# A hybrid decoder layer on one core: the order of the last two experts' weights, the last down projection and the last combination

## The chip, the core and the metric

The kernel runs on one core of one Trainium2 chip. The metric is the device time of one execution in microseconds (us); several executions are timed and the median is given. One execution is also recorded by the hardware profiler; times in it count from the start of its span.

## What is computed

One layer of a decoder for 256 tokens of 2048 channels in float32: a modulated norm, a mixer of a gated recurrence and an attention, an output projection, and then a mixture of 32 experts, of which each token uses two. Only this last part is touched:

```python
g_sel = jnp.argmax(g_logits, axis=-1)                 # 1 of 4 groups
top_val, top_idx = lax.top_k(e_in, 2)                 # 2 of its 8 experts
weights = p_group[:, None] * jax.nn.softmax(top_val, axis=-1)
...
hid = jax.nn.silu(xb @ w_gate[e]) * (xb @ w_up[e])    # 2048 -> 512, twice
return hid @ w_down[e]                                # 512 -> 2048
...
y = jax.ops.segment_sum(contrib, tok, num_segments=T)
x = x + g2[:, None, :] * y
```

Every expert's weights are read once: 8 MB for gate and up, 4 MB for down, in float32.

## The kernel before, in words

**Engines.** TensorE (PE) multiplies and transposes, VectorE (DVE) multiplies and adds, ScalarE (ACT) does activations and issues the stores, SyncE (SP) issues the weight loads. Each takes its instructions in the order of its own list. The build makes that order: it goes by the order of the code, but may put an instruction ahead of earlier ones of the code that still have to wait.

**The weight stream.** All weights come in chunks of up to 128 x 4096 floats (2048 KB) through a ring of seven tiles (4 from the start, 2 and 1 added later). `items` is the hand-written order of the chunks, `ring_fill` (line 154) issues the next loads on SP while a tile is free, `ring_get` names a chunk, and `ring_done` (line 172) gives its tile back, so that a next load can be issued once the matmuls that read it are over. For each expert the order is four up chunks ("gu") and two down chunks ("dn"), the latter each with half of the 2048 output columns.

**An expert.** Its tokens (up to 32) have been gathered by `dispatch` (line 915) for four experts at a time, one step of it after each of the first chunks of an up product. The up product (loop from line 997, matmuls at line 1003) takes 16 matmuls of 256 columns for each chunk; four at a time go to four 32-row parts of one PSUM tile. In float32 each matmul is two instructions in the trace. `hidden` (line 964) makes silu(gate) times up on ACT and DVE, transposes it on PE and copies it to the tile `hT`. `down` (line 974, matmuls at 979) makes half of the output columns for 32 tokens: 16 matmuls of 256 columns and then four DVE multiplies of 32 x 256 with the gate's row (line 983), into 32 rows of `Y4`, which holds the rows of four experts.

**The combination.** When the fourth expert of a group has a half of its columns, `combine` (line 950) multiplies the 128 rows of `Y4` by the tokens' weights `PWT` (transposed): for each block j of 512 columns and each half t of the tokens one matmul (line 956) and one addition of 128 x 512 into the running result `accx` (line 958). In the last group each block is stored when both its additions are done, 512 KB on ACT's queue (line 960). Products and combinations share four PSUM tiles ("w").

**Behind it.** A loop (line 1025) for experts with more than 32 tokens follows; the number of its rounds is read by every engine, and there is no work of it in this trace.

Of the kernel before, what the change touches and what calls it, by code (L numbers as in the profile page):

```python
# [17 lines left out]
P = 128  # L18
D = 2048
# buffers: weight ring, 4 KB tiles that live long, 4 and 2 KB temporaries, splits, more ring later  # L20
RING, NARENA, NTEMP, NSPLIT, RING2 = 4, 14, (8, 6), 4, 2
# rows of w_ada for the gates and the second modulation: chunks behind each step of the products
SPREAD = (1, 4, 7, 5, 5, 2, 0, 0, 0, 2, 1, 1, 0)
EARLY = {28: 1}
HEAD = 2  # expert chunks loaded ahead of the last of these rows
AHEAD = 3  # steps of the first dispatch ahead of the first expert
T = 256
NE = 32
# [5 lines left out]
# column offsets of the shape constants  # L34
# [3 lines left out]
# column offsets of the parameters laid out by channel  # L38
# [7 lines left out]
def tile_hybrid_layer(ctx, tc, A, out):  # L46
# [40 lines left out]
    # ---------------------------------------------------------------- constants  # L87
# [15 lines left out]
    # ---------------------------------------------------------------- weight stream  # L103
# [8 lines left out]
    def merge(ws, bs):  # L112
        """Items ws with the items bs spread behind them."""
        done = 0
        for i, w in enumerate(ws):
            items.append(w)
            want = min(len(bs), -(-(i + 1) * len(bs) // len(ws)))
            items.extend(bs[done:want])
            done = want
# [8 lines left out]
    experts = [(k, e, q) for e in range(NE) for k, q in (("gu", 0), ("gu", 1), ("gu", 2), ("gu", 3), ("dn", 0), ("dn", 1))]  # L128
# [3 lines left out]
    def source(it):  # L132
        k = it[0]
        if k == "adt":
            return A["w_ada_t"][it[1]], 4096
        if k == "ada":
            return A["w_ada"][("g1", "sh2", "sc2", "g2").index(it[1]), it[2]], 4096
        if k == "win":
            if it[2] == (0, 1):
                return A["w_in_1"][it[1]], 3328  # L140
            return A["w_in"][it[1], it[2][0] // 2 - 1], 4096
        if k == "qup":
            return A["w_q_up"][it[1]], 3072
        if k == "kvup":
            return A["w_kv_up"][it[1]], 2048
        if k == "wout":
            return A["w_out"][1 - it[1], it[2]], 4096
        if k == "gu":
            return A["w_gu"][it[1], it[2]], 4096
        return A["w_down"][it[1], it[2]], 4096  # L150
# [26 lines left out]
    # ---------------------------------------------------------------- small helpers  # L177
    def log_exp_tables(inst):
        """The table set with both Ln and Exp, loaded behind inst."""
        load = S.preload_act_table_set("natural_log_exp_and_others")  # L180
        tc.add_manual_dep(load.ins, inst.ins.name, mybir.DependencyInfo(mybir.DependencyClass.NoSync, mybir.DependencyReason.DATA),
                          reason="tables")
# [13 lines left out]
    # ---------------------------------------------------------------- start: x, tables  # L196
# [18 lines left out]
    # silu(c), by channel and as a row on every partition  # L215
# [20 lines left out]
    def adt_chunk(i):  # L236
        """Two tiles of 128 columns of w_ada, transposed, times silu(c)."""
        w = ring_get(("adt", i))
        r = sm(2, "adt")
        for k in range(2):  # L240
            wk = w[:, 2048 * k:2048 * k + 2048]
            with tc.high_priority(-120 if i > 3 else 0):
                V.scalar_tensor_tensor(wk, wk, 1.0, gate, op0=OP.mult, op1=OP.mult, accum_out=r[:, k:k + 1])  # L243
        ring_done(("adt", i))
        mod_shift(sh1[:, i:i + 1], r[:, 0:1], P_BA + i, 1)
        mod_scale(a1[:, i:i + 1], r[:, 1:2], P_BA + 16 + i, P_N1 + i, 1)
# [8 lines left out]
    def ada_chunk(b, ch):  # L255
        """Two K-tiles of silu(c) times a block of 2048 columns of w_ada."""
        w = ring_get(("ada", b, ch))
        if ch == 0:
            acc[b] = psum.tile([P, 512], F32, tag="a", bufs=1, name=nm("pada"))
            V.memset(acc[b], 0.0)  # L260
        for k in range(2):
            kt = 2 * ch + k
            for j in range(4):
                o = D * k + 512 * j
                PE.matmul(acc[b][32 * j:32 * j + 1, :], ca[:, kt:kt + 1], w[:, o:o + 512], start=kt == 0, stop=kt == 15)  # L265
        ring_done(("ada", b, ch))
        if ch == 7:
            ada_end(b)
# [23 lines left out]
    def norm1():  # L292
        """x * rsqrt(mean(x^2) + eps)"""
        ssx = sm(8)
        for j in range(4):
            for t in range(2):
                junk = tmp([P, 512], "junk")
                S.activation(junk, xx[j][:, t], AF.Square, accum_out=ssx[:, 4 * t + j:4 * t + j + 1])
        msx = sm(2)
        V.tensor_reduce(msx, ssx.rearrange("p (t j) -> p t j", t=2), AX.X, OP.add)  # L300
        V.tensor_scalar(msx, msx, 1.0 / D, EPS, op0=OP.mult, op1=OP.add)
        rx = rsqrt(msx, 2)
        for j in range(4):
            for t in range(2):
                V.tensor_scalar(xx[j][:, t], xx[j][:, t], rx[:, t:t + 1], None, op0=OP.mult)

    # rotary tables
# [30 lines left out]
    def make_h(p):  # L338
        """Modulated input of 2 K-tiles, transposed and split."""
# [19 lines left out]
    # lower bound of the forget gates by channel, and its complement  # L359
# [15 lines left out]
    # ---------------------------------------------------------------- dense products in split float32  # L375
    proj = {}

    def dense(wt, ncol, kts, lhs, end, turned=False):
        """A chunk of a dense product; the weights are split into two float32r parts. With turned,
        the channels come out on the partitions: two heads of 256 tokens in a bank."""  # L380
# [51 lines left out]
    def mix_out(ps, gain, hi, lo, t):  # L432
        """Transposed head outputs times their gain, split; ps holds 4 heads of 128 tokens."""
# [5 lines left out]
    def head_rstd(o_sb):  # L439
        """rsqrt of the mean square over each head's 128 columns of o_sb [P, 2, 512]."""  # L440
# [8 lines left out]
    # ---------------------------------------------------------------- gated linear recurrence  # L449
# [83 lines left out]
    # ---------------------------------------------------------------- latent attention  # L533
# [76 lines left out]
    def mla_pre():  # L610
# [35 lines left out]
        # shared rotary key: gain, then rotation  # L646
# [12 lines left out]
    def rot(dst, src, n):  # L659
        """dst, src [P, 2, n, 64]: rotation of the two halves of each 64."""  # L660
# [13 lines left out]
    def mla(g):  # L674
# [11 lines left out]
        def keep(dst, n, o):  # L686
            """Evacuates a product, with the sums of squares of its heads at ss[o:]."""
# [147 lines left out]
    # ---------------------------------------------------------------- router  # L835
# [8 lines left out]
    def first_max(vals, n):  # L844
        """One-hot of the first maximum of vals [P, 2, n], and the maximum [P, 2]."""
# [48 lines left out]
    # rounds beyond the first SL tokens of an expert  # L894
# [10 lines left out]
    # ---------------------------------------------------------------- experts  # L905
    XT, PWT = {}, {}

    def gate_rows():
        """The second gate's row on every partition."""
# [5 lines left out]
    def dispatch(G4):  # L915
        """One-hot rows of 4 experts, then their tokens' columns of the modulated input."""
# [33 lines left out]
    def combine(G4, Y4, js=range(4)):  # L950
        for j in js:
            if G4 == 0:
                accx[j] = big([P, 2, 512], "accx")
            for t in range(2):
                ps = pw("pcmb")
                PE.matmul(ps, PWT[G4][:, 128 * t:128 * t + 128], Y4[j // 2][:, 512 * (j % 2):512 * (j % 2) + 512],  # L956
                          start=True, stop=True)
                V.tensor_add(accx[j][:, t], (x2 if G4 == 0 else accx)[j][:, t], ps)  # L958
            if G4 == 7:
                nc.scalar.dma_start(out[:, :, 512 * j:512 * j + 512], accx[j])  # L960

    H = {}

# [10 lines left out]
    def down(q, w, Y, r):  # L974
        """Half q of the output columns, gated, to rows r of Y."""
# [15 lines left out]
    for e in range(NE):  # L991
# [5 lines left out]
        gu = pm("pgu")  # L997
        for q in range(4):
            w = ring_get(("gu", e, q))
            for i in range(4):  # L1000
                kt = 4 * q + i
                for j in range(4):
                    PE.matmul(gu[32 * j:32 * j + 32, :256], XT[G4][kt // 8][:, kt % 8, 32 * e4:32 * e4 + 32],  # L1003
                              w[:, 1024 * i + 256 * j:1024 * i + 256 * j + 256], start=kt == 0, stop=kt == 15)
            ring_done(("gu", e, q))
            if q < 3 or e == 0:
                next(side, None)
# [5 lines left out]
        hidden(gu)  # L1013
        for q in range(2):
            down(q, ring_get(("dn", e, q)), Y4, 32 * e4)
            ring_done(("dn", e, q))
            if e4 == 3:
                combine(G4, Y4, (2 * q, 2 * q + 1))

    # ---------------------------------------------------------------- experts with more than SL tokens  # L1020
# [72 lines left out]
def _layout(i):  # L1093
# [54 lines left out]
    L["w_down"] = ac(w.transpose(0, 3, 2, 1, 4)).reshape(NE, 2, P, 4096)  # L1148
    return L
# [15 lines left out]
```

## Time and profile before

| | us |
|---|---|
| median of 3 runs | 1505.49 |
| lowest, highest | 1504.41, 1506.1 |
| span of the profiled execution | 1503.6 |

The profile tells for one execution what each engine did. Busy time of a group is the time in which its instructions ran; the idle time behind it is what the engine stood still just before them, with the work that ended most of it (the releaser). Matmuls overlap, so the mean of one is longer than its share of the busy time. PE is the matmul side of TensorE and PEld its weight load, the step that puts the stationary operand in place. L979 is line 979 of the kernel. In the single stretches the columns are the stretch, its length, busy time and number of instructions of PE, PEld, DVE, ACT and POOL, the granted clock of TensorE as a share of 2.4 GHz (0.50 is 1.2 GHz), the busy share of the DMA engines and what they moved in GB/s.

### The profile page before, as it was taken

What the parts mean: (1) busy time and instruction counts of PE and PEld (TensorE: products, weight loads), DVE (VectorE), ACT (ScalarE), POOL (GpSimd) and SP (SyncE); (2) the same over time, 40 slices, a digit from 0 to 9 for tenths busy, and PEclk for the clock granted to TensorE, in tenths of its full rate; (3) what the DMA queues carried; (4) which work ended last, traced back from release to release, by engine and by line L of the source; (5) the groups of instructions that cost most, each with busy time, mean ns of one, the idle gap of its engine ahead of it and who ended that gap; (6) DMA issues with size and microseconds to landing.
All of it is one profiled execution on the core that took longest, in us unless ns stands there. A gap on an engine that the chain in (4) does not pass through costs nothing. (4 is left out here: it accounts for less than half of the span.)

```text
span 1503.6 us, 22669 instructions
## 1 busy us (share of the span) xinstructions
PE 1123.6 (75%) x9813; PEld 686.8 (46%) x9813; DVE 592.3 (39%) x1192; ACT 340.5 (23%) x705; POOL 5.0 (0%) x9
## 2 busy tenths in 40 slices
PE   3799999979999989776667667657667657566555
PEld 1688887637568756333323323323423423333222
DVE  6789998759765552220121121113112112112112
ACT  4564446526435432100100100100100100000000
POOL 0000000000000000000000000000000000000000
PEclk9999999989999999878887888879978888889777
DMA  9788796877979798999999999999999999999995
GB/s 382 314 320 324 284 363 244 332 283 314 367 285 382 295 374 333 429 429 431 430 431 430 429 429 430 430 431 431 430 430 429 430 430 431 431 429 428 431 431 228
DMA packets 43423, 575.61 MB, mean 383 GB/s; under 512 B 4778, under 2 KB 5034, under 8 KB 8376
## 3 DMA queue, kind: packets, MB, share of 16 engines
q1 hardware_dynamic: 41776, 570.56, 91.2%
q10 hardware_dynamic: 1544, 3.56, 0.6%
q8 instruction: 79, 1.29, 0.3%
q14 instruction: 24, 0.20, 0.0%
HBM read 572.00 MB, written 2.11 MB: 382 GB/s over the span
## 5 line engine op out<-in xcount | busy, mean ns | idle before, releaser
L1003 PE MATMUL pgu<-wch,XT 128*32 128x256 f32 x4096 | 314.4, 461 | 188.5 <-DMA wch<-in_w_gu_dram 188.4
L1003 PEld LDWEIGHTS pgu<-wch,XT 128*32 128x32 f32 x4096 | 140.5, 127 | 353.7 <-DMA wch<-in_w_gu_dram 245.1
L979 PE MATMUL py<-wch,hT 128*32 128x256 f32 x2048 | 170.3, 490 | 80.3 <-DMA wch<-in_w_down_dram 73.5
L983 DVE TENSOR_TENSOR Y<-py,gate 32x256 f32<-32x256 f32 x256 | 107.6, 420 | 222.2 <-PE py L979 219.4
L968 DVE TENSOR_TENSOR hid<-sgu,pgu 128x128 f32<-128x128 f32 x32 | 9.2, 288 | 456.2 <-ACT sgu L966 456.2
L386 DVE TENSOR_TENSOR split<-wch,split 128x512 fp32r<-128x512 f32 (+2 forms) x248 | 160.2, 668 | 69.6 <-ACT split L385 68.4
L385 ACT ACTIVATE split<-wch 128x512 fp32r<-128x512 f32 (+2 forms) x248 | 148.1, 615 | 148.5 <-PE pacc L402 99.8
L979 PEld LDWEIGHTS py<-wch,hT 128*32 128x32 f32 x2048 | 80.1, 134 | 158.4 <-issue 63.1
L966 ACT ACTIVATE sgu<-pgu 128x128 f32<-128x128 f32 x32 | 8.9, 278 | 604.4 <-PE pgu L1003 604.4
L938 ACT ACTIVATE XT<-pgat,sh,a 128x128 f32<-128x128 f32 x128 | 48.2, 457 | 219.3 <-PE pgat L933 219.2
L401 PE MATMUL pacc<-split,hhi 128*128 128x512 f32 (+1 forms) x192 | 74.3, 387 | 2.3 <-DVE split L386 2.2
L393 PE MATMUL pacc<-hhi,split 128*128 128x256 f32 x256 | 72.7, 285 | 1.2 <-ACT split L385 1.1
L395 PE MATMUL pacc<-hhi,split 128*128 128x256 f32 x256 | 72.2, 285 | 1.7 <-DVE split L386 1.7
L402 PE MATMUL pacc<-split,hlo 128*128 128x512 f32 (+1 forms) x192 | 73.2, 382 | 0.0
L400 PE MATMUL pacc<-split,hhi 128*128 128x512 f32 (+1 forms) x192 | 71.1, 385 | 2.7 <-ACT split L385 2.7
L394 PE MATMUL pacc<-hlo,split 128*128 128x256 f32 x256 | 72.7, 285 | 0.5 <-DVE hlo L357 0.5
L243 DVE SCALAR_TENSOR_TENSOR wch<-wch,gate 128x2048 f32<-128x2048 f32 x32 | 72.8, 2285 | 0.0
L956 PE MATMUL pcmb<-Y,pwt 128*128 128x512 f32 x128 | 61.2, 622 | 15.5 <-DVE Y L983 15.5
L265 PE MATMUL pada<-wch,ca 128*1 128x512 f32 x512 | 69.9, 608 | 3.8 <-DVE pada L260 3.8
L933 PEld LDWEIGHTS pgat<-ohr,x 128*128 128x128 f32 x512 | 63.3, 205 | 10.4 <-issue 9.4
L933 PE MATMUL pgat<-ohr,x 128*128 128x128 f32 x512 | 66.7, 291 | 0.7 <-DVE sm L900 0.7
L400 PE MATMUL pacc<-split,mhi 128*128 128x512 f32 x128 | 51.0, 400 | 0.0
(301 smaller groups left out, 1187.7 us busy)
## 6 DMA issues: line engine op xcount, KB each, us to landing
wch<-in_w_gu_dram SPq DMA_DIRECT2D x128, 2048.0 KB, 31.1
wch<-in_w_down_dram SPq DMA_DIRECT2D x64, 2048.0 KB, 31.1
wch<-in_w_ada_dram SPq DMA_DIRECT2D x32, 2048.0 KB, 9.6
wch<-in_w_ada_t_dram SPq DMA_DIRECT2D x16, 2048.0 KB, 9.5
wch<-in_w_in_dram SPq DMA_DIRECT2D x16, 2048.0 KB, 9.3
wch<-in_w_out_dram SPq DMA_DIRECT2D x8, 2048.0 KB, 9.6
wch<-in_w_in_dram SPq DMA_DIRECT2D x4, 1664.0 KB, 7.5
x<-in_x_dram SPq DMA_DIRECT2D x8, 512.0 KB, 10.7
```

Source lines behind the costliest of these rows:

```text
L243: V.scalar_tensor_tensor(wk, wk, 1.0, gate, op0=OP.mult, op1=OP.mult, accum_out=r[:, k:k + 1])
L385: S.activation(s[:, 0, :ncol], w, AF.Copy)
L386: V.tensor_sub(s[:, 1, :ncol], w, s[:, 0, :ncol])
L393: PE.matmul(o, s[:, 0, c], hi, start=first and h % 2 == 0, stop=False, skip_group_check=True)
L394: PE.matmul(o, s[:, 0, c], lo, start=False, stop=False, skip_group_check=True)
L400: PE.matmul(o, hi[:, c], s[:, 0, :ncol], start=first, stop=False)
L401: PE.matmul(o, hi[:, c], s[:, 1, :ncol], start=False, stop=False)
L402: PE.matmul(o, lo[:, c], s[:, 0, :ncol], start=False, stop=stop)
L933: PE.matmul(ps[:, 128 * i:128 * i + 128], x2[kt // 4][:, t, 128 * (kt % 4):128 * (kt % 4) + 128], ohr[:, t], start=t == 0, stop=t == 1)
L979: PE.matmul(py[32 * j:32 * j + 32, :256], H["T"][:, 32 * kt:32 * kt + 32], w[:, 1024 * kt + 256 * j:1024 * kt + 256 * j + 256], start=kt = ...
L983: V.tensor_mul(Y[q][r:r + 32, 256 * j:256 * j + 256], py[32 * j:32 * j + 32, :256], gate[32 * j:32 * j + 32, c:c + 256])
L1003: PE.matmul(gu[32 * j:32 * j + 32, :256], XT[G4][kt // 8][:, kt % 8, 32 * e4:32 * e4 + 32], w[:, 1024 * i + 256 * j:1024 * i + 256 * j + 2 ...
```

## The change

The order of the last chunks becomes: the up chunks of experts 30 and 31, the two down chunks of expert 30, then the down weights of expert 31 in four chunks of 1024 KB ("dl", 512 output columns each) from an array of their own, laid out beforehand. Expert 31's up product and hidden step run ahead of expert 30's down product. After each half of that, rows 0 to 95 of `Y4` (experts 28 to 30) are combined. For each quarter of expert 31, `down_quarter` makes 512 columns (16 matmuls of 128 columns, four multiplies of 32 x 128), then rows 96 to 127 are combined for that block, and each token half is stored by itself, one on ACT's queue and one on SP's. The up product of an expert becomes a function of its own (`up`), and comments are gone.

```diff
-    experts = [(k, e, q) for e in range(NE) for k, q in (("gu", 0), ("gu", 1), ("gu", 2), ("gu", 3), ("dn", 0), ("dn", 1))]
+    experts = [(k, e, q) for e in range(NE - 2) for k, q in (("gu", 0), ("gu", 1), ("gu", 2), ("gu", 3), ("dn", 0), ("dn", 1))]
+    experts += [("gu", e, q) for e in (NE - 2, NE - 1) for q in range(4)]
+    experts += [("dn", NE - 2, 0), ("dn", NE - 2, 1)] + [("dl", NE - 1, r) for r in range(4)]
...
+        if k == "dl":
+            return A["w_down_l"][it[2]], 2048
...
-    def combine(G4, Y4, js=range(4)):
+    def combine(G4, Y4, js=range(4), rows=slice(0, P), store=False):
...
-                PE.matmul(ps, PWT[G4][:, 128 * t:128 * t + 128], Y4[j // 2][:, 512 * (j % 2):512 * (j % 2) + 512],
+                PE.matmul(ps, PWT[G4][rows, 128 * t:128 * t + 128], Y4[j // 2][rows, 512 * (j % 2):512 * (j % 2) + 512],
                           start=True, stop=True)
                 V.tensor_add(accx[j][:, t], (x2 if G4 == 0 else accx)[j][:, t], ps)
-            if G4 == 7:
-                nc.scalar.dma_start(out[:, :, 512 * j:512 * j + 512], accx[j])
+                if store:
+                    (nc.scalar if t == 0 else nc.sync).dma_start(out[:, t, 512 * j:512 * j + 512], accx[j][:, t])
...
+    def down_quarter(r, w, Y, hT):
+
+        py = pw("py")
+        for kt in range(4):
+            for j in range(4):
+                PE.matmul(py[32 * j:32 * j + 32, :128], hT[:, 32 * kt:32 * kt + 32],
+                          w[:, 512 * kt + 128 * j:512 * kt + 128 * j + 128], start=kt == 0, stop=kt == 3)
+        for j in range(4):
+            c = 512 * r + 128 * j
+            o = 512 * (r % 2) + 128 * j
+            V.tensor_mul(Y[r // 2][96:128, o:o + 128], py[32 * j:32 * j + 32, :128], gate[32 * j:32 * j + 32, c:c + 128])
...
-    for e in range(NE):
+    for e in range(NE - 1):
...
         hidden(gu)
+        if e == NE - 2:
+            kept = H["T"]
+            hidden(up(NE - 1, lambda: None))
+            last, H["T"] = H["T"], kept
         for q in range(2):
             down(q, ring_get(("dn", e, q)), Y4, 32 * e4)
             ring_done(("dn", e, q))
             if e4 == 3:
                 combine(G4, Y4, (2 * q, 2 * q + 1))
+            elif e == NE - 2:
+                combine(G4, Y4, (2 * q, 2 * q + 1), rows=slice(0, 96))
+    for r in range(4):
+        down_quarter(r, ring_get(("dl", NE - 1, r)), Y4, last)
+        ring_done(("dl", NE - 1, r))
+        combine(7, Y4, (r,), rows=slice(96, 128), store=True)
```

## Rows read from the trace of the kernel before

**Rows 1.** The page: busy time of the engines, and GB/s moved in 40 equal slices

```profile
PE 1123.6 (75%) x9813; PEld 686.8 (46%) x9813; DVE 592.3 (39%) x1192; ACT 340.5 (23%) x705; POOL 5.0 (0%) x9
...
GB/s 382 314 320 324 284 363 244 332 283 314 367 285 382 295 374 333 429 429 431 430 431 430 429 429 430 430 431 431 430 430 429 430 430 431 431 429 428 431 431 228
```

**Rows 2.** The page: the costliest groups of instructions, expert products

```profile
L1003 PE MATMUL pgu<-wch,XT 128*32 128x256 f32 x4096 | 314.4, 461 | 188.5 <-DMA wch<-in_w_gu_dram 188.4
...
L979 PE MATMUL py<-wch,hT 128*32 128x256 f32 x2048 | 170.3, 490 | 80.3 <-DMA wch<-in_w_down_dram 73.5
```

**Rows 3.** Timeline, PE: start, length, instruction and count, idle before and releaser

```profile
1462.70 3.64 PE L1003 MATMUL pgu<-wch,XT 128*32 128x256 f32 x32 [2.15 <-DMA wch<-in_w_gu_dram]
...
1467.54 3.64 PE L1003 MATMUL pgu<-wch,XT 128*32 128x256 f32 x32 [1.20 <-DMA wch<-in_w_gu_dram]
...
1472.39 3.45 PE L1003 MATMUL pgu<-wch,XT 128*32 128x256 f32 x32 [1.21 <-DMA wch<-in_w_gu_dram]
...
1477.22 1.93 PE L1003 MATMUL pgu<-wch,XT 128*32 128x256 f32 x32 [1.39 <-DMA wch<-in_w_gu_dram]
...
1482.16 3.52 PE L979 MATMUL py<-wch,hT 128*32 128x256 f32 x32 [1.95 <-SPq L1025]
```

**Rows 4.** Single microseconds: busy times of the engines, granted clock, DMA share, GB/s

```profile
1473.00:1474.00 1.00, 1.00 (x16) 0.41 (x10) 0.00 (x0) 0.00 (x0) 0.00 (x0) 0.50 0.88 377
...
1485.00:1486.00 1.00, 0.67 (x8) 0.00 (x0) 0.28 (x1) 0.00 (x0) 0.00 (x0) 0.62 0.27 115
1486.00:1487.00 1.00, 0.38 (x1) 0.30 (x2) 0.96 (x3) 0.00 (x0) 0.00 (x0) 1.00 0.00 0
```

**Rows 5.** Timeline of the end, PE and DVE

```profile
1486.62 3.70 PE L956 MATMUL pcmb<-Y,pwt 128*128 128x512 f32 x8 [0.95 <-DVE Y L983]
...
1490.25 1.93 PE L979 MATMUL py<-wch,hT 128*32 128x256 f32 x32
...
1492.25 1.75 DVE L983 TENSOR_TENSOR Y<-py,gate 32x256 f32<-32x256 f32 x4 [1.21 <-PE py L979]
1493.16 3.70 PE L956 MATMUL pcmb<-Y,pwt 128*128 128x512 f32 x8 [0.97 <-DVE Y L983]
...
1496.90 0.69 DVE L958 TENSOR_TENSOR accx<-accx,pcmb 128x512 f32<-128x512 f32 x1 [0.17 <-PE pcmb L956]
```

**Rows 6.** DMA issues: operation, count, KB each, median us from issue to landing

```profile
wch<-in_w_down_dram SPq DMA_DIRECT2D x64, 2048.0 KB, 31.1
...
out_dram<-accx ACTq DMA_DIRECT2D x4, 512.0 KB, 3.4
```

**Rows 7.** Timeline, PE, at experts 0 and 25

```profile
585.14 0.33 PE L970 MATMUL phT<-cst,hid 128*128 128x128 f32 x1 [0.72 <-DVE hid L968]
585.40 0.62 PE L1003 MATMUL pgu<-wch,XT 128*32 128x256 f32 x2
585.85 3.65 PE L979 MATMUL py<-wch,hT 128*32 128x256 f32 x64
...
1285.89 1.93 PE L1003 MATMUL pgu<-wch,XT 128*32 128x256 f32 x32 [1.32 <-DMA wch<-in_w_gu_dram]
1287.76 3.84 PE L933 MATMUL pgat<-ohr,x 128*128 128x128 f32 x32
```

**Rows 8.** Timeline, PE, at the end of the group before the last

```profile
1366.88 3.70 PE L956 MATMUL pcmb<-Y,pwt 128*128 128x512 f32 x8 [0.96 <-DVE Y L983]
```

**Rows 9.** A matmul of one row, and groups of DVE multiplies by their shape

```profile
556.53 3.74 PE L912 MATMUL pg<-brows,cst 1*128 1x512 f32 x8 [0.79 <-DVE brows L274]
...
L983 DVE TENSOR_TENSOR Y<-py,gate 32x256 f32<-32x256 f32 x256 | 107.6, 420 | 222.2 <-PE py L979 219.4
...
L968 DVE TENSOR_TENSOR hid<-sgu,pgu 128x128 f32<-128x128 f32 x32 | 9.2, 288 | 456.2 <-ACT sgu L966 456.2
```

**Rows 10.** Timeline, weight loads of PE in a product at half and at full clock

```profile
1462.70 0.20 PEld L1003 LDWEIGHTS pgu<-wch,XT 128*32 128x32 f32 x8 [3.03 <-DMA wch<-in_w_gu_dram]
...
1490.25 1.45 PEld L979 LDWEIGHTS py<-wch,hT 128*32 128x32 f32 x32 [0.76 <-DVE accx L958]
```

More of the change, by code (lines that the diff above doesn't have):

```diff
@@ L955, in combine, with up @@
                 ps = pw("pcmb")
-                PE.matmul(ps, PWT[G4][:, 128 * t:128 * t + 128], Y4[j // 2][:, 512 * (j % 2):512 * (j % 2) + 512],
+                PE.matmul(ps, PWT[G4][rows, 128 * t:128 * t + 128], Y4[j // 2][rows, 512 * (j % 2):512 * (j % 2) + 512],
                           start=True, stop=True)
                 V.tensor_add(accx[j][:, t], (x2 if G4 == 0 else accx)[j][:, t], ps)
-            if G4 == 7:
-                nc.scalar.dma_start(out[:, :, 512 * j:512 * j + 512], accx[j])
+                if store:
+                    (nc.scalar if t == 0 else nc.sync).dma_start(out[:, t, 512 * j:512 * j + 512], accx[j][:, t])
     H = {}
+    def up(e, next_step):
+        G4, e4 = divmod(e, 4)
+        gu = pm("pgu")
+        for q in range(4):
+            w = ring_get(("gu", e, q))
+            for i in range(4):
+                kt = 4 * q + i
+                for j in range(4):
+                    PE.matmul(gu[32 * j:32 * j + 32, :256], XT[G4][kt // 8][:, kt % 8, 32 * e4:32 * e4 + 32],
+                              w[:, 1024 * i + 256 * j:1024 * i + 256 * j + 256], start=kt == 0, stop=kt == 15)
+            ring_done(("gu", e, q))
+            if q < 3 or e == 0:
+                next_step()
+        return gu
+    def down_quarter(r, w, Y, hT):
[4 more added lines that the diff above has]
+                          w[:, 512 * kt + 128 * j:512 * kt + 128 * j + 128], start=kt == 0, stop=kt == 3)
+        for j in range(4):
+            c = 512 * r + 128 * j
+            o = 512 * (r % 2) + 128 * j
+            V.tensor_mul(Y[r // 2][96:128, o:o + 128], py[32 * j:32 * j + 32, :128], gate[32 * j:32 * j + 32, c:c + 128])
     def hidden(gu):
@@ L996, in tile_hybrid_layer @@
             side = dispatch(G4 + 1)
[L997 to L1007, printed above, removed]
+        gu = up(e, lambda: next(side, None))
         if e == 0:
@@ L1148, in _layout @@
     L["w_down"] = ac(w.transpose(0, 3, 2, 1, 4)).reshape(NE, 2, P, 4096)
+    w = np.asarray(i["w_down"])[0][NE - 1].reshape(4, P, 4, 512)
+    L["w_down_l"] = ac(w.transpose(2, 1, 0, 3)).reshape(4, P, 2048)
     return L
```

## The prediction

> **What bounds the kernel now.** I read the busy shares first: TensorE is busy 75% of the span and no engine is full [rows 1]. That is an average over stages, so the second view is the costliest groups of instructions. In the expert stage both big products spend their idle time on a weight load [rows 2]: this stage runs at the pace of the transfers. The third view is the timeline of the last 60 us. A weight chunk of 2048 KB lands every 4.84 us (products start at 1462.70, 1467.54, 1472.39, 1477.22), and PE waits for each one [rows 3]. The last product in this row starts at 1482.16; its releaser is named as the queue of SP, but one more step of 4.84 us from 1477.22 is 1482.06, so I read it as the landing of the last expert's first down half. The fourth view, single microseconds, shows the transfers ending: they still move data in 1485 to 1486 and none in 1486 to 1487 [rows 4]. So the last weights are there by 1486.0, while the last addition ends at 1496.90 + 0.69 = 1497.59 [rows 5]. From 1482.16 on the end is set by PE's own chain: half of the down product, two of four multiplies, eight combination matmuls, and all of that again [rows 5]. After the last addition comes a store of 512 KB that lands in 3.4 us [rows 6], and the span ends at 1503.6, 6.0 us behind that addition.
>
> The span of 1503.6 is 1.9 us below the median of 1505.49. I make the sum against the span and carry its difference to the median.
>
> **The order of arrival.** The reordering brings no byte less. Expert 31's four up chunks move ahead of expert 30's two down chunks, so the latter take the places of 1472.4 and 1477.2, and four transfers of half the size come at 2.42 us each after them, the last by 1486.0 as before. The hidden step of expert 31 (two activations, a multiply and a transpose, hidden today behind a load) goes between two landings and stays hidden: its chunk lands at about 1467.5, and a product takes at most 3.64 us [rows 3]. On SP the last issues wait for ring slots; a load is on its way for about 31 us [rows 6], 6 to 7 chunks, so a slot that holds half a chunk still leaves over 15 us queued. Cost 0; without that cover a hole would be as long as the missing half chunk, 2.4 us.
>
> **What it adds on PE.** Today expert 30's down products run in the shadow of loads and its rows are combined together with those of the last expert. Now they stand at the end, and the combination is done twice: 16 instructions for rows 0 to 95 and 16 for rows 96 to 127. Fewer rows don't make a matmul shorter: eight instructions with one row and 512 columns took 3.74 us, eight with 128 rows 3.70 us [rows 5, 9]. So the second set costs as much as the first.
>
> The sum starts at the landing at 1472.4, in us on PE:
> - expert 30, first half: 3.45. At this place today's product runs at half clock [rows 3, 4] and the pattern of loads ahead of it is the same; at full clock it would be 1.93 [rows 5].
> - the wait for two multiplies: 0.95 [rows 5]; nothing else has landed to fill it.
> - combination of two column blocks: 1490.25 - 1486.62 = 3.63 [rows 5].
> - second half: 1.93 [rows 5].
> - the next wait of 0.95 is filled by the first narrow product: 1.2 (below).
> - the second pair of blocks: 3.63.
> - three more narrow products: 3.6.
> - four narrow combinations of half a pair each: 4 x 1.82 = 7.28.
> - to the last addition 0.11 (1496.90 against 1493.16 + 3.63) and the addition 0.69: 0.8 [rows 5].
>
> Together 26.5 us, so the last addition ends at 1498.9, against 1497.6: +1.3 us.
>
> **Narrow product.** No row has it: 32 instructions with 128 columns in place of 256. Bounds: half the wide one's 1.86 us (1.93 less the overlap with what follows), 0.93, if the columns set it; 1.86 if something else does. Between them lies the weight load: 32 loads of 32 columns are busy for 1.45 us in a wide product, but eight of them took 0.20 us where none had to wait for a matmul [rows 10], which is 0.8 us for 32. I take 1.2, halfway between these two. The Trainium skill (TensorE: Matmul & The Clock Gate, section "LDWEIGHTS (loading the stationary operand)") says that a load takes its column count divided by 1.2 in ns; as an estimate from that page 32 loads are 0.85 us, and the product would be bound by its columns. By that rule the sum would be 1.1 us lower; the eight loads agree with it, the 1.45 us don't.
>
> **The waits inside the quarters.** Each narrow combination needs four multiplies of 32x128. A multiply of 128 columns took 288 ns, one of 256 columns 420 ns [rows 9]; four are 1.16 us, plus 0.14 us from product to multiply (1492.25 - 1490.25 - 1.86 [rows 5]): 1.3 us. In code order PE would stand idle for that in each quarter. I cost it at nothing, because the next quarter's product can cover it: by then its weights are long there. That PE's order leaves the code's order for such gaps is seen: after expert 0's transpose two matmuls of expert 1's up product run ahead of expert 0's down product, which waits for an activation [rows 7]; and 32 gather matmuls of two steps run in one stretch although the code puts an up chunk between them [rows 7].
>
> DVE gets 8 wide multiplies (3.4 us), 16 narrow ones (4.6) and 16 additions (11.0) from 1475.9 on, 19.0 us, done by 1494.9 if never waiting: it stays behind PE. The PSUM tiles of the products and combinations are four; the one that a narrow product takes was read by an addition two products earlier.
>
> **Stores.** The last store is 256 KB rather than 512, on SP or ACT. At some 430 GB/s, the rate of the last stage [rows 1], 512 KB take 1.2 us, so I take 0.6 us off; bounds 0 (the landing time doesn't depend on size) and 1.7 (half of 3.4). The six earlier halves and the more issues, under 0.4 us each, lie beside PE's chain. SP now has to leave its list after its last store as ACT does today; both stores leave within one addition of each other.
>
> Net: +1.3 - 0.6 = +0.7 us: span 1504.3, median 1505.49 + 0.7 = **1506.2**. With the first half at full clock 1.5 less, with a narrow product of 0.93 or 1.86 us 1.1 less or 2.6 more, with the store's bounds 1.1 less or 0.6 more: its own range is 1502.5 to 1509.4.
>
> **Rivals.**
> 1. PE keeps the code's order, slower. Place: PE between narrow product and narrow combination. Price: 0.95 for the gap ahead of the second pair and 4 x 1.3 for the quarters, 6.15 us: 1512.4; with part of the gaps filled, between. It decides when the build, at the moment it orders these matmuls, does not yet count the next transfer as landed. For it: at the ends of earlier groups the gap of 0.96 us ahead of the combination stayed empty [rows 8]. Against it: there the next chunk had 4.84 us to come, here 2.42, and PE is behind. Chance 0.25.
> 2. The last transfer sets the end, faster, as the smaller pieces would have it. Then: 1486.0 + 1.34 + 1.2 + 1.82 + 0.8 = 1491.2, 6.4 us earlier, with the store 7.0: 1498.5. It decides if PE is done with all else by 1486.0. Against it: between 1472.4 and then lie 13.6 us, and the sum puts over 20 us of work ahead of the last quarter. For it: only that part of this work might run side by side, since the two combinations use different rows. Chance 0.07.
> 3. Narrow products at the pace of their columns, 0.93 us: 1505.1, the mechanism otherwise that of the forecast. For it: the eight quick loads [rows 10]. The rule on weight loads above is this case. Chance 0.16.
>
> **How the numbers follow.** The forecast has 0.52. What a measurement here can tell from no change is about 0.2%, 3.0 us: below 1502.5 is faster, above 1508.5 slower. Faster: rival 2 and 0.02 from the low end of the others, 0.09. Slower: rival 1 and 0.06 from the forecast's upper end (wide-priced narrow products), 0.31. The rest, 0.60, is no change. The range of 1503.0 to 1513.0 holds the forecast and rival 3 but for 0.04, and over half of rival 1: a little over 0.8.
>
> **What would show it.** Right: expert 30's down product starts at about 1472.4 of the span; PE is idle under 2 us in total between then and its last matmul; a narrow product of quarter 1 or later stands ahead of the combination of the quarter before; narrow combinations take 1.7 to 1.9 us; the last addition is 0 to 3 us later than now. Wrong: idle gaps of over 1 us ahead of each narrow combination (rival 1), PE waiting on a transfer after 1480 (rival 2), an expert 30 product that starts later than 1474 (a hole in the loads), or a store that lands slower from SP.

## The result, and the profile after

The changed kernel takes 1517.73 us (median of 4 runs, 1516.92 to 1518.34) against 1504.95 for the one before: ratio 1.0085, 95% interval 1.0073 to 1.0098, 12.8 us slower. The span of the profiled execution is 1515.7 us, against 1503.6.

The timeline of the end, PE and the last addition of DVE (start, length, instruction, count, idle before and its releaser):

```profile
1472.57 3.41 PE L1011 MATMUL py<-wch,hT 128*32 128x256 f32 x32
...
1476.95 3.70 PE L960 MATMUL pcmb<-Y,pwt 96*128 96x512 f32 x8 [0.97 <-DVE Y L1015]
...
1480.58 1.93 PE L1011 MATMUL py<-wch,hT 128*32 128x256 f32 x32
...
1483.48 3.70 PE L960 MATMUL pcmb<-Y,pwt 96*128 96x512 f32 x8 [0.97 <-DVE Y L1015]
...
1487.12 1.08 PE L989 MATMUL py<-wch,hT 128*32 128x128 f32 x32
...
1489.52 1.98 PE L960 MATMUL pcmb<-Y,pwt 32*128 32x512 f32 x4 [1.32 <-DVE Y L994]
...
1491.43 1.08 PE L989 MATMUL py<-wch,hT 128*32 128x128 f32 x32
...
1493.83 1.98 PE L960 MATMUL pcmb<-Y,pwt 32*128 32x512 f32 x4 [1.32 <-DVE Y L994]
...
1495.73 1.65 PE L989 MATMUL py<-wch,hT 128*32 128x128 f32 x32
...
1498.68 3.78 PE L960 MATMUL pcmb<-Y,pwt 32*128 32x512 f32 x4 [1.30 <-DVE Y L994]
...
1502.39 1.94 PE L989 MATMUL py<-wch,hT 128*32 128x128 f32 x32
...
1505.64 3.77 PE L960 MATMUL pcmb<-Y,pwt 32*128 32x512 f32 x4 [1.32 <-DVE Y L994]
...
1509.45 0.69 DVE L962 TENSOR_TENSOR accx<-accx,pcmb 128x512 f32<-128x512 f32 x1 [1.02 <-PE pcmb L960]
```

Two things are to be seen. First, the list is in the order of the code: product, wait of 1.3 us, combination, four times over. Second, the same work takes twice as long in the last two quarters: a narrow combination 1.98 us and then 3.78. The four quarters as stretches, from one narrow product to the next and the last to its last addition (length; busy time of PE, PEld, DVE, ACT, POOL; granted clock; DMA share; GB/s):

```profile
1487.12:1491.43 4.31, 2.99 (x38) 1.47 (x37) 2.54 (x6) 0.00 (x0) 0.00 (x0) 1.00 0.02 4
1491.43:1495.73 4.30, 2.98 (x37) 1.47 (x36) 2.53 (x6) 0.00 (x0) 0.00 (x0) 1.00 0.32 122
1495.73:1502.39 6.66, 5.36 (x38) 2.36 (x37) 2.54 (x6) 0.00 (x0) 0.00 (x0) 0.53 0.21 81
1502.39:1509.45 7.06, 5.71 (x37) 2.53 (x36) 2.53 (x6) 0.00 (x0) 0.00 (x0) 0.50 0.20 79
```

The granted clock falls from 1.00 to 0.50 at the third quarter, from 2.4 to 1.2 GHz. DVE's share of each quarter stays at 2.5 us.

Where the 12.1 us of span went: the last addition ends at 1509.45 + 0.69 = 1510.14, 12.55 us later than before [rows 5]. Had the last two quarters gone like the second, the fourth product would have started at 1495.73 + 4.30 = 1500.03 and the last addition ended 5.1 us behind it (this distance is 5.11 us in run e3 below, at full clock): 1505.1. So 5.0 us are the clock and 7.5 us are work and waits. In this trace the store gives 0.45 us back: from the last addition to the end of the span it is 5.56 us now and was 6.01 (other runs below give back less). The DMA issues have the halves land sooner too (KB each, median us to landing), against 3.4 us for 512 KB [rows 6]:

```profile
wch<-in_w_down_l_dram SPq DMA_DIRECT2D x4, 1024.0 KB, 25.4
...
out_dram<-accx ACTq DMA_DIRECT2D x4, 256.0 KB, 2.5
out_dram<-accx SPq DMA_DIRECT2D x4, 256.0 KB, 2.5
```

### The profile page after: what moved, and what is told of

Same layout as the page of the kernel before. It is cut to its first block, busy times and chain, and to the rows that moved or that the text cites. A ratio compares the mean times of both kernels' runs of the same rounds, so it can differ in the third digit from the quotient of the medians.

```text
span 1515.7 us, 22860 instructions
## 1 busy us (share of the span) xinstructions
PE 1130.0 (75%) x9893; PEld 690.9 (46%) x9893; DVE 599.1 (40%) x1208; ACT 340.5 (22%) x705; POOL 5.0 (0%) x9
## 4 chain that ended last, share of the span: by engine, by line
DMA 49%; PE 39%; DVE 9%; ACT 2%; issue 1%; SPq 0%; ACTq 0%
DMA wch<-in_w_gu_dram 35%; DMA wch<-in_w_down_dram 12%; PE pacc L405 5%; PE pgu L977 5%; PE pacc L404 5%; PE pacc L406 5%; PE pcmb L960 4%; PE pada L269 3%; PE py L1011 3%; DVE wch L247 2%; PE pgat L937 1%; DVE split L390 1%; PE pacc L399 1%; PE pacc L397 1%; PE pacc L398 1%
## 5 line engine op out<-in xcount | busy, mean ns | idle before, releaser
L1011 PE MATMUL py<-wch,hT 128*32 128x256 f32 x1984 | 161.2, 481 | 77.6 <-DMA wch<-in_w_down_dram 75.0
L1015 DVE TENSOR_TENSOR Y<-py,gate 32x256 f32<-32x256 f32 x248 | 104.2, 420 | 211.5 <-PE py L1011 208.7
L1011 PEld LDWEIGHTS py<-wch,hT 128*32 128x32 f32 x1984 | 76.3, 133 | 151.6 <-issue 62.5
L960 PE MATMUL pcmb<-Y,pwt 128*128 128x512 f32 (+2 forms) x144 | 74.7, 663 | 20.7 <-DVE Y L1015 15.5
L960 PEld LDWEIGHTS pcmb<-Y,pwt 128*128 128x128 f32 (+2 forms) x144 | 28.2, 208 | 59.8 <-issue 28.4
```

The source lines that it names most:

```text
L960: PE.matmul(ps, PWT[G4][rows, 128 * t:128 * t + 128], Y4[j // 2][rows, 512 * (j % 2):512 * (j % 2) + 512], start=True, stop=True)
L1011: PE.matmul(py[32 * j:32 * j + 32, :256], H["T"][:, 32 * kt:32 * kt + 32], w[:, 1024 * kt + 256 * j:1024 * kt + 256 * j + 256], start=kt = ...
L1015: V.tensor_mul(Y[q][r:r + 32, 256 * j:256 * j + 256], py[32 * j:32 * j + 32, :256], gate[32 * j:32 * j + 32, c:c + 256])
```

## The experiments

The runs of a group (e1 to e4, e5 to e8, e9 and e10) share their runs of the kernel before; a difference between groups is taken from each run's distance to those. Spans are of the profiled execution.

### One part alone: the reordering (e4)

```diff
-    ... + [("dl", NE - 1, r) for r in range(4)]
+    ... + [("dn", NE - 1, q) for q in range(2)]
...
-            elif e == NE - 2:
-                combine(G4, Y4, (2 * q, 2 * q + 1), rows=slice(0, 96))
...
+    H["T"] = last
+    for q in range(2):
+        down(q, ring_get(("dn", NE - 1, q)), Y4, 96)
+        ring_done(("dn", NE - 1, q))
+        combine(7, Y4, (2 * q, 2 * q + 1), store=True)
```

> The reordering alone: expert 31's up chunks and hidden step ahead of expert 30's down chunks, but the last down projection in two transfers as before, one combination over 128 rows and the stores as before. If the loss lies in the quarters and the split combination: the last down half lands at the same time, the chain behind it is the same, span 1503.6 within 1 us. Rival (the reordering itself opens a hole in the loads or delays expert 30): over 1505, and expert 30's first down product later than 1474 of the span.

Measured: 1505.09 us against 1504.73, ratio 1.0004 (0.9995 to 1.0014), span 1502.6. Expert 30's first down product starts at 1470.95. The reordering alone costs nothing and gives nothing that these runs can tell: the interval includes a ratio of 1.

### Why the list stays in code order (e1)

```diff
     def down_quarter(r, w, Y, hT):
-        py = pw("py")
+        py = pm("py")
```

`pw` hands out the four PSUM tiles that products and combinations share, `pm` the three of the up products, gathers and transposes.

> The changed kernel with one word changed: the narrow products take their PSUM tiles from the other set (the three tiles of the up products) and no longer from the four that they shared with the combinations. Theory 1 (the products stayed behind their neighbours because of those four tiles): PE's list now has the products in pairs ahead of the combinations, of the four waits of 1.32 us at most two short ones are left, the clock stays at 1.00, so 4 to 5 us for the clock and about 4 us for the waits go: span about 1506 (1505 to 1508). Rival (my own condition of rival 1: the build did not count the next transfer as landed): the list stays in code order, span 1515.7 within 1 us.

Measured: 1511.16 against 1504.73 us, ratio 1.0040 (1.0026 to 1.0055), span 1507.7. The narrow products now stand in pairs ahead of the combinations (timeline, PE):

```profile
1486.47 1.96 PE L989 MATMUL py<-wch,hT 128*32 128x128 f32 x64
...
1488.87 4.09 PE L960 MATMUL pcmb<-Y,pwt 32*128 32x512 f32 x8 [0.45 <-DVE Y L994]
...
1492.89 3.18 PE L989 MATMUL py<-wch,hT 128*32 128x128 f32 x64
...
1496.14 4.53 PE L960 MATMUL pcmb<-Y,pwt 32*128 32x512 f32 x8
```

One word changed the list, so the four shared PSUM tiles held the products back, and the condition that I gave for rival 1 (the next transfer is not yet counted as landed) falls: the transfers are the same in both. The waits in the quarters are down to one of 0.45 us. The span of 1507.7 lies inside theory 1's range, but 1.7 us above its 1506, and one part of the theory failed: the clock did not stay at 1.00 (the same columns as above):

```profile
1486.00:1492.00 6.00, 5.55 (x74) 3.09 (x72) 5.04 (x13) 0.00 (x0) 0.00 (x0) 1.00 0.07 26
1492.00:1496.00 4.00, 4.00 (x66) 2.72 (x64) 2.19 (x6) 0.00 (x0) 0.00 (x0) 0.57 0.70 228
1496.00:1498.50 2.50, 2.42 (x10) 1.14 (x7) 2.27 (x7) 0.00 (x0) 0.00 (x0) 1.00 0.00 0
1498.50:1501.00 2.50, 2.18 (x4) 0.36 (x2) 1.32 (x3) 0.00 (x0) 0.00 (x0) 0.57 0.74 272
```

PE was busy for 5.55 of 6 us and the clock fell behind that. It came back during the second pair of products and fell again in the second set of combinations, whose eight instructions took 4.53 us. So little idle time makes idle time an unlikely cause here; e5 below has the same idle time and keeps the clock.

### What the clock fell for (e2, e3)

Two matmuls on constants behind each narrow product, result unused:

```diff
+        pf = pm("pf")
+        for n in (512, 128):
+            fill = PE.matmul(pf[:, :n], ident, cst[:, 0:n], start=True, stop=True)
...
         combine(7, Y4, (r,), rows=slice(96, 128), store=True)
```

> The changed kernel with two matmuls on constants (512 and 128 columns, 1.1 us at full clock, their result unused) behind each narrow product, where PE waited 1.32 us. The order is otherwise unchanged. Theory 2 (the idle time in the waits lets the clock fall to half in the third quarter): the clock stays at 1.00 to the last matmul, all four quarters take about 4.3 us in place of 4.31, 4.30, 6.66 and 7.06, span about 1510.7. Rival (the clock falls because the combination's matmuls use 32 rows only): the third and fourth quarter stay at 6.7 to 7.1 us, span 1515 to 1517.

Measured: 1511.99 against 1504.73 us, ratio 1.0046 (1.0029 to 1.0063), span 1509.7. Product, filler and combination of the third quarter, and the clock over all four:

```profile
1494.50 1.08 PE L989 MATMUL py<-wch,hT 128*32 128x128 f32 x32
...
1495.51 1.35 PE L1053 MATMUL pf<-cst 128*128 128x512 f32 x4
...
1496.90 1.98 PE L960 MATMUL pcmb<-Y,pwt 32*128 32x512 f32 x4
```

```profile
1486.00:1503.00 17.00, 16.83 (x160) 8.49 (x157) 10.05 (x24) 0.00 (x0) 0.00 (x0) 1.00 0.25 94
```

The four quarters take 4.31 us each, and work that computes nothing makes the kernel nearly 6 us faster than the change alone. The fillers fill the wait, but they also are matmuls over 128 rows, so this run alone does not say which of the two holds the clock. The next one does: the waits stay, and the last combinations use all 128 rows, with weights of zero for rows 0 to 95.

```diff
+    pz = moe.tile([P, 256], F32, tag="pz", bufs=1, name=nm("pz"))
+    V.memset(pz, 0.0)
+    V.tensor_copy(pz[96:128], PWT[7][96:128])
+    PWT[7] = pz
...
-        combine(7, Y4, (r,), rows=slice(96, 128), store=True)
+        combine(7, Y4, (r,), store=True)
```

> The changed kernel with the last four combinations over all 128 rows of Y, with weights of zero for rows 0 to 95, so that the result is the same. Waits and count of matmuls stay. Theory 2 (idle time): the clock falls in the third quarter as before, span 1515.7 within 1 us. Rival (32 rows): the clock stays at 1.00, the third and fourth quarter take 4.3 us, span about 1510.7.

Measured: 1512.05 against 1504.73 us, ratio 1.0048 (1.0032 to 1.0065), span 1508.6:

```profile
1493.38 1.08 PE L989 MATMUL py<-wch,hT 128*32 128x128 f32 x32
...
1495.78 1.98 PE L960 MATMUL pcmb<-Y,pz 128*128 128x512 f32 x4 [1.32 <-DVE Y L994]
...
1497.70 1.08 PE L989 MATMUL py<-wch,hT 128*32 128x128 f32 x32
...
1502.12 0.69 DVE L962 TENSOR_TENSOR accx<-accx,pcmb 128x512 f32<-128x512 f32 x1 [0.17 <-PE pcmb L960]
```

```profile
1484.75:1501.00 16.25, 10.97 (x143) 5.76 (x143) 9.45 (x23) 0.00 (x0) 0.00 (x0) 1.00 0.26 98
```

PE is idle for a third of this stretch (10.97 of 16.25 us busy) and waits 1.32 us in each quarter as in the changed kernel, and the clock stays at 1.00. My theory 2 falls and the rival stands: matmuls of the same count, length (at full clock) and spacing lost the clock with 32 rows and kept it with 128.

### Both losses taken away (e5)

The edits of e1 and e3 together.

> The products in the other set of PSUM tiles and the last combinations over 128 rows, both edits together on the changed kernel: the case that my forecast described, order loosened and clock at full. Theory: the two losses add, so with both gone the forecast's sum holds, span 1504.3 to 1506, and the change is within 0.2% of before, no gain. Rival (something third costs, or the two losses were one and the same): over 1507, or the clock falls again.

Measured: 1508.25 against 1505.93 us, ratio 1.0016 (1.0007 to 1.0025), span 1506.0. PE's rows, from the second early combination on, and the clock over the two pairs of quarters:

```profile
1483.56 3.70 PE L960 MATMUL pcmb<-Y,pwt 96*128 96x512 f32 x8 [0.97 <-DVE Y L1015]
...
1487.19 1.95 PE L989 MATMUL py<-wch,hT 128*32 128x128 f32 x64
...
1489.60 3.70 PE L960 MATMUL pcmb<-Y,pz 128*128 128x512 f32 x8 [0.45 <-DVE Y L994]
...
1493.23 1.96 PE L989 MATMUL py<-wch,hT 128*32 128x128 f32 x64
...
1495.62 3.70 PE L960 MATMUL pcmb<-Y,pz 128*128 128x512 f32 x8 [0.44 <-DVE Y L994]
```

```profile
1487.00:1493.00 6.00, 5.55 (x73) 3.12 (x72) 5.03 (x13) 0.00 (x0) 0.00 (x0) 1.00 0.11 44
1493.00:1500.00 7.00, 5.88 (x73) 3.12 (x72) 5.86 (x14) 0.00 (x0) 0.00 (x0) 1.00 0.59 190
```

The clock holds. That is a second pair of runs in which only the rows differ: e1 and e5 have the same order of the list and in the first pair of quarters the same 5.55 us of work in 6 us, and only e1, with 32 rows, loses the clock behind it.

The last addition ends at 1500.05, and the kernel is 2.3 us slower than before. This is the case that the forecast described, and its 0.7 us was short by 1.6. The list leaves three waits, 0.97 us ahead of the second pair of blocks and twice 0.45 us, 1.87 us in all. The four narrow products take 3.91 us in place of 4.8, which gives half of that back. The other part is the store: from the last addition to the end of the span it is 5.95 us, where the forecast had 6.0 less 0.6.

### Without the early combination (e6, e7, e8)

```diff
-            elif e == NE - 2:
-                combine(G4, Y4, (2 * q, 2 * q + 1), rows=slice(0, 96))
...
-        combine(7, Y4, (r,), rows=slice(96, 128), store=True)
+        combine(7, Y4, (r,), store=True)
```

> The changed kernel without the early combination: rows 0 to 127 are combined once, behind each quarter; reordering, quarters and halved stores stay, the list in code order. Theory: the early combination is 13.9 us of PE work that stood between 1472.6 and 1487.1; without it the first quarter starts when its chunk lands (about 1479.6), four quarters take 4.31 us each at full clock, the last addition ends at 1497.7, span 1503.5 (1502.5 to 1505), so no gain and no loss against before. Rival (the loss lies in the quarters themselves, their waits and their clock): the clock falls in the third quarter here too, over 1506.

Measured: 1507.95 against 1505.93 us, ratio 1.0010 (1.0000 to 1.0019), span 1505.9. The clock fell here too, though in the first quarter, where PE waits for chunks, and not in the third:

```profile
1480.33 1.08 PE L989 MATMUL py<-wch,hT 128*32 128x128 f32 x32 [0.58 <-DMA wch<-in_w_down_l_dram]
...
1482.81 3.51 PE L960 MATMUL pcmb<-Y,pwt 128*128 128x512 f32 x4 [1.40 <-DVE Y L994]
```

That is 1.5 us over the 1.98 of a combination at full clock (granted 0.66 over 1482 to 1487); my sum had left it out, and the span missed the range that I gave. The chain starts when the first quarter lands and not 6.8 us later, so the early combination is what pushed the quarters back (1487.12 - 1480.33). Its price comes from runs that differ in it alone: e3 is 7.3 us above its kernel before and e6 2.0, so 5.3 us; with the products in the other tiles e5 is 2.3 us above and e7 (next) 1.3 below, so 3.6 us.

Adding e1's word to this:

> As the run before, with the narrow products in the other set of PSUM tiles, so that a product may run ahead of the combination of the quarter before. Theory: the transfers set the pace up to the last landing at about 1486, then one product, two combinations and the addition are left: last addition at 1493 to 1495, span 1499 to 1501, 2.5 to 4.5 us below before. Rival (PE still sets the end, the pulled products wait for their chunk and hold up the combination behind them): no better than the run before, 1503.5.

Measured: 1504.60 against 1505.93 us, ratio 0.9991 (0.9982 to 1.0000), span 1502.7; the last addition starts at 1495.95, so it ends 1.6 us behind the range that I gave, again with a slow first combination (3.43 us). The span and the gain of 1.3 us miss what I gave for them too.

The same with the loads in the order of the kernel before:

> The run before without the reordering: expert 30's down chunks ahead of expert 31's up chunks as in the kernel before, and the last down projection in four transfers, one combination over 128 rows for each quarter, products in the other PSUM tiles. If the reordering pays because it takes the hidden step out of the end: 1 to 1.5 us slower than the run before (its first product waits for the hidden step, 1480.7 in place of 1479.6). Rival (the reordering does nothing for the end): the same as the run before within 0.5 us.

Measured: 1505.68 against 1505.93 us, ratio 0.9996 (0.9987 to 1.0005), span 1503.7. The 1.1 us between e7 and e8 have the sign and size expected for the hidden step, but the two intervals overlap: it stays open whether the reordering pays.

### Each product one quarter ahead, without and with fillers (e9, e10)

e7 with each product one quarter ahead of the combination in the code (e9), and with fillers at two places, behind expert 30's last down product and behind the first quarter's product (e10). The edit of e10; `fill` issues two matmuls on constants, and in e9 the first three lines are `quarter(0)` alone:

```diff
+    pf = pm("pf")
+    fill(lastdn)
+    fill(quarter(0))
     for r in range(4):
-        down_quarter(r, ring_get(("dl", NE - 1, r)), Y4, last)
-        ring_done(("dl", NE - 1, r))
+        if r < 3:
+            quarter(r + 1)
         combine(7, Y4, (r,), store=True)
```

> A version drawn from the runs: reordering, quarters, one combination over 128 rows for each quarter, products in the other PSUM tiles, and in the code each product one quarter ahead of the combination. Against the run e7 the first combination no longer depends on where the build places it. Theory: the same stretch as there, with the clock falling in the sparse time between 1478 and 1484: span 1501 to 1503, 1 to 3 us below before. Rival: the combination now stands behind products that wait for their chunk, no gain against before.

> The same with two matmuls on constants (512 and 128 columns, result unused) behind expert 30's last down product and behind the first quarter's product, where PE waits for the next chunk. Theory: they keep the clock at 1.00, the first combination takes 1.98 us in place of about 3.4, last addition near 1494, span 1499 to 1501, 3 to 5 us below before. Rival (the fillers stand in the way, or the clock isn't what costs there): the same as e9 or slower.

Measured: e9 1504.45 against 1505.55 us, ratio 0.9992 (0.9983 to 1.0001), span 1501.6. Its clock, around the wait for the second quarter's chunk:

```profile
1478.00:1481.00 3.00, 1.18 (x36) 0.84 (x32) 2.73 (x8) 0.00 (x0) 0.00 (x0) 1.00 0.50 213
1481.00:1485.00 4.00, 3.83 (x35) 2.54 (x36) 1.33 (x6) 0.00 (x0) 0.00 (x0) 0.57 0.44 182
```

e10: 1502.80 against 1505.55 us, ratio 0.9983 (0.9974 to 0.9992), span 1499.5:

```profile
1481.97 1.08 PE L989 MATMUL py<-wch,hT 128*32 128x128 f32 x32
1482.98 1.98 PE L960 MATMUL pcmb<-Y,pwt 128*128 128x512 f32 x4
...
1488.83 3.70 PE L960 MATMUL pcmb<-Y,pwt 128*128 128x512 f32 x8
...
1492.57 0.69 DVE L962 TENSOR_TENSOR accx<-accx,pcmb 128x512 f32<-128x512 f32 x1 [0.17 <-PE pcmb L960]
```

```profile
1476.00:1493.00 17.00, 15.99 (x184) 8.34 (x184) 12.49 (x31) 0.00 (x0) 0.00 (x0) 1.00 0.55 211
```

With the clock held the first combination takes 1.98 us and the last addition ends at 1493.26. e9's interval includes a ratio of 1, so it is not shown to be faster than the kernel before. e10 is 2.75 us (0.17%) faster, a little under the 3 us that I gave, and about 15 us faster than the change. The 1.65 us between e9 and e10 have the sign expected, but their intervals overlap. The fillers add busy time and use all 128 by 128 of the array, so, as with e2, which of the two held the clock is not shown. e10 keeps the reordering and the quarters and drops the early combination; whether the reordering adds to it was not run.

## Why the prediction was wrong, point by point

- **What bounds the end: right.** PE's own chain set it, not the last transfer. Rival 2 fell, as its own objection said: in all runs with the early combination the first quarter's product started at 1484 to 1488, with its weights long there. (Its sum has 1.34 us for the wait that is 1.3 elsewhere, which changes nothing.)
- **The terms on PE: right within 0.2 us each.** Expert 30's first half 3.41 us (3.45), the pair of combinations 3.63 (1480.58 - 1476.95), the second half 1.93, the narrow combination 1.91 (1491.43 - 1489.52, forecast 1.82), the wait 1.32 (1.3). The narrow product is 1.08 us where I took 1.2. Its 32 weight loads took this long:

```profile
1487.11 0.81 PEld L989 LDWEIGHTS py<-wch,hT 128*32 128x32 f32 x32 [0.76 <-issue]
```

  The figure of the Trainium skill (TensorE: Matmul & The Clock Gate, "LDWEIGHTS (loading the stationary operand)"), 0.85 us for 32 loads as an estimate from that page, agrees. The same 32 loads are busy for 1.45 us in a wide product [rows 10]; the loads alone don't need that, and I gave it half a say. Where two products stand together they take 1.96 us (e1), 0.98 each: rival 3's 0.93 was nearer than my 1.2, by a term of 0.1 to 0.2 us for each quarter.
- **The step that failed first:** "I cost it at nothing, because the next quarter's product can cover it", with the sentence on the four PSUM tiles as its cover. The code does say that products and combinations share four tiles; I looked at whether a tile would be free in time on the chip, and not at whether the order of the list could come out that way. In place of nothing PE stood idle for 0.97 us ahead of the second pair and for 1.3 us in each quarter, 6.2 us in all. The rows that I leaned on [rows 7] show work that moves ahead from another set of tiles (up products and gathers), and the row against [rows 8] was one with products and combinations. Rival 1 had this at 0.25 and at 6.15 us; by its own price the last addition would be 7.45 us later than before, and at full clock it is 7.5. Its condition was wrong: e1 shows the tiles, not the transfers. Even with other tiles 1.87 us of waits are left (e5).
- **The step that was missing:** the clock. The forecast took half clock for the first product and full clock behind it, and no case let it fall again. That is 5.0 us of the 12.55, and it is why the time lies above the range's end of 1513.0, which rival 1 nearly filled alone (1512.4).
- **Stores: right only in part.** In the changed kernel 0.45 us are saved, forecast 0.6. But from the last addition to the end of the span it is 5.79 us in e3 and 5.95 in e5, against 6.01 before and 6.11 in e4, whose stores are whole: with the quarters in pairs, the case of the forecast, only 0.06 us are saved.
- **The direction:** even with both losses gone (e5) the change is 0.16% slower, within what the forecast called no change. No run of this form of it shows a gain: with the early combination the first quarter's product starts at 1487.12, without it at 1480.33 (e6), when its weights land, and the early combination costs 3.6 to 5.3 us.

## What to carry to other kernels

Work split so that it can start earlier is paid on the engine that does it: a combination over 96 rows costs as much as one over 128, and if that engine sets the end, splitting loses. Before counting on a later product to fill a wait, look at which buffers the two share: here the tile set of the products decided the order of the list. And cost a tail at both levels of the clock.

## What the runs showed of the hardware that I had not expected

The granted clock fell behind a stretch in which PE was busy for 5.55 of 6 us (e1) and stayed at 1.00 behind one with the same 5.55 of 6 us (e5); it fell to 0.50 in the changed kernel and stayed at 1.00 in e3, with PE busy for only 10.97 of 16.25 us. Within each of these two pairs the matmuls of the combination were as many, as far apart and, at full clock, as long (1.98 us for four instructions with 32 rows and with 128); where the clock fell they used 32 rows of the array, where it stayed 128. So narrow operands cost nothing in their own time here and cost the clock of what followed. In e3 and e5 the 96 added rows carry weights of zero, so whether it is the number of rows or which rows, no run here shows, nor which part of the chip decides.

Rows are not the only thing that goes with a fall: in e9 no matmul of the end uses fewer than 128 rows, PE was busy for 1.18 of 3 us while it waited for a chunk, and the clock over the next 4 us was 0.57.
